# Joining a head's attention and carry products, and loading the Nyquist weights with a repeated source

## The chip, the cores and the metric

The kernel runs on one core of a Trainium2 chip. The metric is the device time of one execution in microseconds (us). Engines are called TensorE (PE in the profile, its weight loads PEld), VectorE (DVE), ScalarE (ACT), GpSimd (POOL) and SyncE (SP, whose queue issues nearly all DMAs).

## The reference

One layer of a diffusion backbone for 128 context tokens and 256 latent tokens, width 2048, all in float32. Cut to what matters here:

```python
# adaLN: shift, scale and gate vectors from SiLU(cond) @ w_ada, for both sub-layers
h = rmsnorm(x, norm_pre_mix) * (1 + sc1) + sh1
q, k, v, g, lr_f, lr_b, fo = split(h @ w_in)
# branch A: gated linear attention, 4 heads, both directions, in chunks of 64 tokens
b = cumsum(log_a); total = b[last]
q_in, k_in, k_out = q * exp(b), k * exp(-b), k * exp(total - b)
att = where(mask, q_in @ k_in.T, 0)         # within a chunk
o = att @ v + q_in @ state                  # state carried from chunk to chunk
state = state * exp(total) + k_out.T @ v
# branch B: real part of a 2-D DFT over positions and the 256 channels of each of 4 groups
f = fft2(fo.reshape(t, 4, 256), axes=(positions, channels)).real
merged = sigmoid(gate_a) * (norm(o) * silu(g) @ w_br_gla) + sigmoid(gate_b) * (f @ w_br_four)
x = x + ga1 * rmsnorm(merged @ w_out)
x = x + ga2 * rmsnorm(swiglu_ffn(rmsnorm(x) * (1 + sc2) + sh2))
# outputs: x of both token kinds, and the final context states of both directions
```

## The kernel before

All 384 tokens go through the layer together, and activations lie transposed: channels on partitions, tokens in the free dimension. A large product is done as three float32r products of split operands (high x high, high x low, low x high). The helper `gemm` issues them (line 257), 24 for a weight tile of 128 x 1024. Such a tile is loaded by SP (`load`, L196, tile raw, 2 buffers), and split by `split`: ScalarE copies the high part (L224, whi), VectorE subtracts the low part (L225, wlo), 4 buffers each. `grab` takes a finished tile and starts the load and split of a later one. `proj` makes one output tile of 128 channels from two weight tiles, and after each of the two it calls `step(side)`, which runs one piece of side work up to its next `yield`. The order on TensorE, ScalarE, VectorE and GpSimd is the order of the program (`manual_schedule`); the order of SP's queue is left to the scheduler until the last stage.

The stages that the change touches are two.

**GLA.** While the 32 gate projections run, the side work is `gla()` with the generator `ada_rest` beside it, one step of each after every weight tile. `ada_rest` multiplies the remaining adaLN weights on VectorE (L530, tile adacc, about 2.5 us a step); every 18 steps it has two products on TensorE: pr (L538) and, one step later, ptm (L547). For each of 4 heads, `gla` makes kr, the decay exponents (z, la, bT, sx), per direction d the tiles qi, ki, ko, kc (VectorE, L661 to L668), and then in three steps: the attention products of direction 0 (at, L684), those of direction 1 (at again), and the carry products from chunk to chunk (cr, L704). Each of these is 6 small products with 64 output rows, plain float32, so that the profile shows 12 records of each. VectorE copies at under a mask into att (L687), for direction 1 by way of the tile am (L694, L697), and ScalarE copies cr into att (L708). Later steps split att, ko and q, and make the state products dl and the outputs po. All of these results lie in the PSUM pool `pss` of 5 tiles (tag side), which are handed out in turn.

**Fourier branch.** After GLA, 8 projections make the Fourier channels (fo), two for each of 4 groups. The second of a pair makes sum and difference of both (fs, VectorE, L898 and L899). The side work `dft()` then does the DFT over channels with the constants cd: px (L844, L845) one step later, then pp (L830). The Nyquist channel has its own row pnr and its own weights wn, which `four` uses (L943) once for each of 16 output tiles. wn holds 128 x 2048 values, of which rows 0 to 3, 32 to 35 and 64 to 67 are filled: the same four weight rows three times, as high, low and high part. `nyq_weights(h)` makes one half: GpSimd clears a tile wr (L868), SP loads its 12 rows by 12 DMAs (L873), each 8 pieces of 128 floats; in the next step ScalarE copies wr to wn (L876) and VectorE subtracts for the low rows (L877). wr shares its buffer (tag ws, one buffer) with the tile in which `fold` adds up the weights of `w_br_four`. After each of the first four projections one step of it is run.

Of the kernel before, what the change touches and what calls it, by code (L numbers as in the profile page):

```python
# [11 lines left out]
F32 = mybir.dt.float32  # L12
# [8 lines left out]
P = 128  # L21
# [5 lines left out]
CH = 64  # L27
# [69 lines left out]
def tile_step(ctx: ExitStack, tc: tile.TileContext, a, o):  # L97
    nc = tc.nc
    PE, ACT, DVE, POOL, SP = nc.tensor, nc.scalar, nc.vector, nc.gpsimd, nc.sync
# [215 lines left out]
    pss = ctx.enter_context(tc.tile_pool(name="pss", bufs=5, space=PSUM))  # L315
    with ExitStack() as s:
# [126 lines left out]
        for kb in range(KT):  # L443
# [17 lines left out]
            hf = scr[:, kb % 8, :]  # L461
# [42 lines left out]
        for t in range(3):  # L504
# [5 lines left out]
            for g in range(2):  # L510
                cs = slice(512 * g, 512 * g + 512)
# [58 lines left out]
    with ExitStack() as s:  # L570
        pg = s.enter_context(tc.tile_pool(name="pg", bufs=1))
# [8 lines left out]
        for c in range(2):  # L580
            src = a["a2"][:, 512 * c : 512 * c + 512]
# [3 lines left out]
        mask = pg.tile([P, 2, CH], U32, name="mask")  # L585
        ss = pg.tile([P, 3, 4], F32, name="ss")

        def hf(c):
            return slice(64 * (c % 2), 64 * (c % 2) + 64)
# [4 lines left out]
        def gla():  # L594
# [10 lines left out]
            for h in range(NH):  # L605
# [33 lines left out]
                for d in range(2):  # L639


                    bT = pss.tile([P, T], F32, tag="side", name="bT")
                    for t in range(3):
                        for j, l in enumerate((lah, lal)):
                            PE.matmul(
                                bT[:, t * P : (t + 1) * P], l[:, t, d], tri[:, d * P : (d + 1) * P],
                                start=j == 0, stop=j == 1,
                            )
                    sx = pss.tile([P, 2, P], F32, tag="side", name="sx")
                    for j, l in enumerate((lah, lal)):  # L650
                        PE.matmul(
                            sx, tri[:, (2 + d) * P : (3 + d) * P], l[:, 0 : 2 + d : 1 + d, d], start=j == 0, stop=j == 1,
                        )
                    eb = pg.tile([P, T], F32, tag=f"eb{d}", name="eb")
                    ACT.activation(eb, bT, AF.Exp)
                    ki = pg.tile([P, T], F32, tag=f"ki{d}", name="ki")
                    ACT.activation(ki, bT, AF.Exp, scale=-1.0)
                    ko = pg.tile([P, 2, P], F32, tag=f"ko{d}", name="ko")
                    ACT.activation(ko, sx, AF.Exp)
                    qi = pg.tile([P, T], F32, tag=f"qi{d}", name="qi")  # L660
                    DVE.scalar_tensor_tensor(qi, eb, DK**-0.5, qT[:, h, :], op0=ALU.mult, op1=ALU.mult)  # L661
                    DVE.tensor_mul(ki, ki, kT[:, h, :])
                    DVE.tensor_mul(ko, ko, krs[:, 0 : 2 + d : 1 + d, :])

                    last = 0 if d else CH - 1
                    tot = chunks(eb)[:, :, d, last : last + 1]
                    kc = pg.tile([P, 3, CH], F32, tag=f"kc{d}", name="kc")
                    DVE.tensor_mul(kc, chunks(ki)[:, :, d, :], tot.to_broadcast([P, 3, CH]))  # L668
                    dc = pg.tile([P, 1], F32, tag=f"dc{d}", name="dc")
                    c = 5 if d else 2  # L670
                    e0, e1 = c * CH + last, (c + 1 - 2 * d) * CH + last
                    DVE.tensor_mul(dc, eb[:, e0 : e0 + 1], eb[:, e1 : e1 + 1])
                    qin.append(qi)
                    kin.append(ki)
                    kcr.append(kc)
                    kout.append(ko)
                    dec.append((tot, dc))
                    yield
                for d in range(2):
                    qi, ki = qin[d], kin[d]  # L680
                    at = pss.tile([P, 3, CH], F32, tag="side", name="at")
                    for c in range(6):
                        cs = slice(c * CH, (c + 1) * CH)
                        PE.matmul(at[hf(c), c // 2, :], ki[:, cs], qi[:, cs], start=True, stop=True)  # L684
                    if d == 0:
                        for c in range(2):
                            DVE.copy_predicated(  # L687
                                att[hf(c), :, c * CH : (c + 1) * CH],
                                mask[hf(c), 0:1, :].to_broadcast([CH, 3, CH]), at[hf(c)],
                            )  # L690
                    else:
                        am = pg.tile([P, 3, CH], F32, tag="am", name="am")
                        POOL.memset(am, 0.0)
                        DVE.copy_predicated(am, mask[:, 1:2, :].to_broadcast([P, 3, CH]), at)  # L694
                        for c in range(2):
                            v = att[hf(c), :, c * CH : (c + 1) * CH]
                            DVE.tensor_add(v, v, am[hf(c)])  # L697
                    yield

                cr = pss.tile([P, 3, CH], F32, tag="side", name="cr")  # L700
                for t in range(3):
                    for d in range(2):
                        c = 2 * t + 1 - d
                        PE.matmul(  # L704
                            cr[hf(d), t, :], kcr[d][:, t, :], qin[d][:, c * CH : (c + 1) * CH], start=True, stop=True,
                        )
                for d in range(2):
                    ACT.copy(att[hf(d), :, (1 - d) * CH : (2 - d) * CH], cr[hf(d)])  # L708
                for d in range(2):
# [93 lines left out]
    with ExitStack() as s:  # L803
# [57 lines left out]
            DVE.tensor_sub(pnr[64:96], pn[64:96], pnr[64:96].bitcast(F32))  # L861
            yield

        def nyq_weights(h):

            n = D // 2
            wr = pc.tile([P, n], F32, tag="ws", name="wr")
            POOL.memset(wr, 0.0)  # L868
            for g in range(4):
                src = a["w_br_four"][8 * h : 8 * h + 8, 32 * g : 32 * g + 1, (2 * g + 1) * P : (2 * g + 2) * P]  # L870
                for j in range(3):
                    r = 32 * j + g
                    SP.dma_start(wr[r : r + 1, :].rearrange("p (i c) -> p i c", c=P), src.rearrange("i p c -> p i c"))  # L873
            yield
            w = wn[:, n * h : n * h + n]
            ACT.copy(w, wr)  # L876
            DVE.tensor_sub(w[32:64], wr[32:64], w[32:64].bitcast(F32))  # L877
            yield

        df = dft()  # L880

# [4 lines left out]
                yield  # L886

        sd = side()
        nw = (u for h in range(2) for u in nyq_weights(h))
        rate[0] = 0.7  # L890
        for i in range(8):
            def fo(p, i=i):
                if i % 2 == 0:
                    fs[i // 2] = pc.tile([P, 2, T], F32, tag="fs", name="fs", bufs=2)
                    ACT.copy(fs[i // 2][:, 0, :], p)
                else:
                    f = fs[i // 2]
                    DVE.tensor_sub(f[:, 1, :], f[:, 0, :], p)  # L898
                    DVE.tensor_add(f[:, 0, :], f[:, 0, :], p)  # L899
                    done[0] = i + 1  # L900

            proj(psm, hT, fo, sd)
            if i < 4:
                next(nw)

        gates, raw_gates = {}, []
        gorder = iter([u for u in mix_order if u[0] != "o"])
# [424 lines left out]
```

## Time and profile before

| what | value |
|---|---|
| time, median of 3 runs | 2057.03 us (2055.79 to 2059.26) |
| the profiled execution's own time | 2056.04 us |
| its span, first to last instruction | 2054.3 us |
| TensorE busy | 2024.7 us, 99% of the span |
| VectorE, ScalarE, GpSimd busy | 1274.9, 770.1, 45.4 us |
| granted TensorE clock | 0.994 of full speed |
| GLA heads lie in | about 200 to 480 us |
| Fourier projections lie in | about 510 to 590 us |

A row of a timeline gives start, length, engine, line, operation, output and inputs, count, and in brackets how long the engine sat idle before it and what ended that. Matmuls are pipelined, so their lengths overlap; what one costs is read from start to start. A row of a tile or line gives the count, least, median and greatest length in ns, and the first and last start. SPq is the time in which SP issues a DMA.

### The profile page before, as it was taken

The numbers are of one execution on the slowest core, as the hardware profiler recorded it, in microseconds if no ns is written. First come the engines' busy times: TensorE is split into PE (matmuls) and PEld (weight loads), VectorE is DVE, ScalarE is ACT, GpSimd is POOL, SyncE is SP. The second block draws the span as 40 slices with busy tenths as digits, with TensorE's granted clock in tenths as the row PEclk, the third lists the DMA queues.
The fourth block names the chain that finished last, engine by engine and source line by source line (L and its number), as shares of the span: only waits on it lengthen the run. The fifth ranks groups of instructions, "written<-read, shape, count | busy, mean of one in ns | idle before, by whom it ended". The sixth has DMA issues, their size and how long they took to land.

```text
span 2054.3 us, 30097 instructions
## 1 busy us (share of the span) xinstructions
PE 2024.7 (99%) x12214; PEld 1956.1 (95%) x12214; DVE 1274.9 (62%) x1663; ACT 770.1 (37%) x1143; POOL 45.4 (2%) x52
## 2 busy tenths in 40 slices
PE   8999999999999999999999999999999999999998
PEld 5779999999999999978999999999999999999996
DVE  5669787898667778867444555553545454544346
ACT  3233545453346544445333322222222322222234
POOL 0000000000000000022000000000000000000001
PEclk9999999999999999999999999999999999999998
DMA  9978677767646785532444444443444444433332
GB/s 387 354 261 274 206 238 230 240 222 259 202 158 209 257 282 183 187 113 93 154 144 152 146 144 154 144 146 125 150 144 147 151 144 148 148 125 124 123 133 83
DMA packets 112563, 373.94 MB, mean 182 GB/s; under 512 B 13860, under 2 KB 32484, under 8 KB 108328
## 3 DMA queue, kind: packets, MB, share of 16 engines
q1 hardware_dynamic: 111560, 370.84, 52.8%
q8 instruction: 96, 1.57, 0.3%
q10 hardware_dynamic: 864, 1.18, 0.2%
q14 instruction: 43, 0.35, 0.1%
HBM read 358.34 MB, written 13.63 MB: 181 GB/s over the span
## 4 chain that ended last, share of the span: by engine, by line
PE 96%; DVE 2%; DMA 1%; ACT 1%; issue 0%; SPq 0%; DVEq 0%; ACTq 0%
PE pmm L257 66%; PE pdn L257 18%; PE pv L391 3%; PE pf L257 2%; PE pgm L374 1%; PE px L409 1%; DVE yE L1227 0%; PE po L603 0%; PE pmm L1131 0%; DMA Clo<-in_xT 0%; PE pr L538 0%; DMA slab<-in_w_ada 0%; DVE z L1090 0%; PE dl L603 0%; PE px L844 0%
## 5 line engine op out<-in xcount | busy, mean ns | idle before, releaser
L257 PE MATMUL pmm<-A_hi,whi 128*128 128x384 f32 x2480 | 832.6, 336 | 0.0
L257 PE MATMUL pmm<-A_hi,wlo 128*128 128x384 f32 x2480 | 828.9, 334 | 0.0
L257 PE MATMUL pmm<-A_lo,whi 128*128 128x384 f32 x2480 | 828.8, 334 | 0.0
L225 DVE TENSOR_TENSOR wlo<-raw,whi 128x1024 fp32r<-128x1024 f32 x433 | 529.0, 1223 | 433.8 <-ACT whi L224 432.9
L224 ACT CAST whi<-raw 128x1024 fp32r<-128x1024 f32 x436 | 457.7, 1050 | 587.4 <-PE pmm L257 223.2
L257 PEld LDWEIGHTS pmm<-A_hi,whi 128*128 128x128 f32 x2480 | 465.6, 188 | 3.4 <-issue 1.8
L257 PEld LDWEIGHTS pmm<-A_lo,whi 128*128 128x128 f32 x2480 | 465.7, 188 | 0.2
L257 PEld LDWEIGHTS pmm<-A_hi,wlo 128*128 128x128 f32 x2480 | 465.6, 188 | 0.0
L530 DVE SCALAR_TENSOR_TENSOR adacc<-adaw,spad,adacc 128x1024 f32<-128x1024 f32 x240 | 296.9, 1278 | 0.6 <-DMA adaw<-in_w_ada 0.3
L257 PE MATMUL pdn<-hid_hi,whi 128*128 128x384 f32 x704 | 235.2, 334 | 0.0
L257 PE MATMUL pdn<-hid_hi,wlo 128*128 128x384 f32 x704 | 235.1, 334 | 0.0
L257 PE MATMUL pdn<-hid_lo,whi 128*128 128x384 f32 x704 | 235.1, 334 | 0.0
L257 PEld LDWEIGHTS pdn<-hid_hi,whi 128*128 128x128 f32 x704 | 132.2, 188 | 0.4 <-issue 0.4
L257 PEld LDWEIGHTS pdn<-hid_lo,whi 128*128 128x128 f32 x704 | 132.2, 188 | 0.0
L257 PEld LDWEIGHTS pdn<-hid_hi,wlo 128*128 128x128 f32 x704 | 132.2, 188 | 0.0
L283 ACT CAST hid_hi<-hfE 128x384 fp32r<-128x384 f32 x44 | 22.6, 513 | 161.6 <-DVE hfE L1154 161.6
L1154 DVE TENSOR_TENSOR hfE<-sg,pmm 128x384 f32<-128x384 f32 x44 | 24.4, 555 | 82.2 <-PE pmm L257 81.6
L1146 ACT ACTIVATE sg<-pmm 128x384 f32<-128x384 f32 x44 | 21.6, 492 | 133.5 <-PE pmm L257 133.5
L1171 DVE TENSOR_TENSOR Blo<-Blo,pdn 128x384 f32<-128x384 f32 x72 | 39.5, 553 | 46.6 <-PE pdn L257 46.6
L1171 DVE TENSOR_TENSOR Bhi<-Bhi,pdn 128x384 f32<-128x384 f32 x72 | 39.0, 549 | 34.0 <-PE pdn L257 34.0
L257 PE MATMUL pmm<-o_hi,whi 128*128 128x384 f32 x128 | 42.8, 335 | 0.0
L257 PE MATMUL pmm<-o_lo,whi 128*128 128x384 f32 x128 | 42.8, 334 | 0.0
(301 smaller groups left out, 1556.9 us busy)
## 6 DMA issues: line engine op xcount, KB each, us to landing
adaw<-in_w_ada SPq DMA_DIRECT2D x128, 512.0 KB
raw<-in_w_g SPq DMA_DIRECT2D x88, 512.0 KB
raw<-in_w_u SPq DMA_DIRECT2D x88, 512.0 KB
raw<-in_w_d SPq DMA_DIRECT2D x88, 512.0 KB
slab<-in_w_ada SPq DMA_DIRECT2D x32, 1024.0 KB
raw<-in_w_gate SPq DMA_DIRECT2D x64, 512.0 KB
raw<-in_w_in SPq DMA_DIRECT2D x44, 512.0 KB
raw<-in_w_out SPq DMA_DIRECT2D x32, 512.0 KB
```

The costliest lines, as they stand in the source:

```text
L224: ACT.copy(hi, raw)
L225: eng.tensor_sub(lo, raw, hi.bitcast(F32))
L257: PE.matmul(dst, w[wi][:, k * n + n0 : k * n + n0 + P], x[xi][:, k0 + k, :], start=first and k == 0 and j == 0, stop=last and k == kts - 1 ...
L283: ACT.copy(hi, src)
L374: PE.matmul(pgv[q : q + 32, :], spad[:, k, :], slab[k // (KT // 2)][:, k % (KT // 2), :], start=k < 4, stop=k >= KT - 4,)
L391: PE.matmul(pv[2 * t + g], hT[x_][:, kb, t * P : (t + 1) * P], w_[:, g * 512 : (g + 1) * 512], start=kb == 0 and j == 0, stop=kb == KT - 1 ...
L409: PE.matmul(px, w_[:, u * P : (u + 1) * P], hT[x_][:, kb, :], start=j == 0, stop=j == 2)
L530: DVE.scalar_tensor_tensor(acc[:, c, :], w, spad[:, k, c : c + 1], acc[:, c, :], op0=ALU.mult, op1=ALU.add,)
L1146: ACT.activation(sgs[j], p, AF.Silu)
L1154: DVE.tensor_mul(hf, sgs.pop(j), p)
L1171: DVE.tensor_add(acc(k), acc(k), p)
```

## The change

In `gla`, the 12 attention products of both directions and the 6 carry products are issued in one step, one after the other on TensorE. The work of the other engines on them keeps its three steps; the number of steps of a head stays the same. In the Fourier branch, each half of the Nyquist weights is loaded by four DMAs, each of which reads a weight row once for each of three target rows 32 partitions apart (a source with a repeated dimension). Two of them are issued in one step and two in the next, and the copy follows in a third, so that both halves take six steps, after the first six projections.

```diff
@@ -676,26 +676,13 @@
                     kout.append(ko)
                     dec.append((tot, dc))
                     yield
+
+                ats = []
                 for d in range(2):
-                    qi, ki = qin[d], kin[d]
-                    at = pss.tile([P, 3, CH], F32, tag="side", name="at")
+                    ats.append(pss.tile([P, 3, CH], F32, tag="side", name="at"))
                     for c in range(6):
                         cs = slice(c * CH, (c + 1) * CH)
-                        PE.matmul(at[hf(c), c // 2, :], ki[:, cs], qi[:, cs], start=True, stop=True)
-                    if d == 0:
-                        for c in range(2):
-                            DVE.copy_predicated(
-                                att[hf(c), :, c * CH : (c + 1) * CH],
-                                mask[hf(c), 0:1, :].to_broadcast([CH, 3, CH]), at[hf(c)],
-                            )
-                    else:
-                        am = pg.tile([P, 3, CH], F32, tag="am", name="am")
-                        POOL.memset(am, 0.0)
-                        DVE.copy_predicated(am, mask[:, 1:2, :].to_broadcast([P, 3, CH]), at)
-                        for c in range(2):
-                            v = att[hf(c), :, c * CH : (c + 1) * CH]
-                            DVE.tensor_add(v, v, am[hf(c)])
-                    yield
+                        PE.matmul(ats[d][hf(c), c // 2, :], kin[d][:, cs], qin[d][:, cs], start=True, stop=True)
 
                 cr = pss.tile([P, 3, CH], F32, tag="side", name="cr")
                 for t in range(3):
@@ -704,6 +691,19 @@
                         PE.matmul(
                             cr[hf(d), t, :], kcr[d][:, t, :], qin[d][:, c * CH : (c + 1) * CH], start=True, stop=True,
                         )
+                for c in range(2):
+                    DVE.copy_predicated(
+                        att[hf(c), :, c * CH : (c + 1) * CH],
+                        mask[hf(c), 0:1, :].to_broadcast([CH, 3, CH]), ats[0][hf(c)],
+                    )
+                yield
+                am = pg.tile([P, 3, CH], F32, tag="am", name="am")
+                POOL.memset(am, 0.0)
+                DVE.copy_predicated(am, mask[:, 1:2, :].to_broadcast([P, 3, CH]), ats[1])
+                for c in range(2):
+                    v = att[hf(c), :, c * CH : (c + 1) * CH]
+                    DVE.tensor_add(v, v, am[hf(c)])
+                yield
                 for d in range(2):
                     ACT.copy(att[hf(d), :, (1 - d) * CH : (2 - d) * CH], cr[hf(d)])
                 for d in range(2):
@@ -861,21 +861,24 @@
             DVE.tensor_sub(pnr[64:96], pn[64:96], pnr[64:96].bitcast(F32))
             yield
 
-        def nyq_weights(h):
+        def nyq_weights():
 
             n = D // 2
-            wr = pc.tile([P, n], F32, tag="ws", name="wr")
-            POOL.memset(wr, 0.0)
-            for g in range(4):
-                src = a["w_br_four"][8 * h : 8 * h + 8, 32 * g : 32 * g + 1, (2 * g + 1) * P : (2 * g + 2) * P]
-                for j in range(3):
-                    r = 32 * j + g
-                    SP.dma_start(wr[r : r + 1, :].rearrange("p (i c) -> p i c", c=P), src.rearrange("i p c -> p i c"))
-            yield
-            w = wn[:, n * h : n * h + n]
-            ACT.copy(w, wr)
-            DVE.tensor_sub(w[32:64], wr[32:64], w[32:64].bitcast(F32))
-            yield
+            for h in range(2):
+                wr = pc.tile([P, n], F32, tag="ws", name="wr")
+                POOL.memset(wr, 0.0)
+                for g in range(4):
+                    src = a["w_br_four"][8 * h : 8 * h + 8, 32 * g : 32 * g + 1, (2 * g + 1) * P : (2 * g + 2) * P]
+                    SP.dma_start(
+                        wr[g : g + 65 : 32, :].rearrange("p (i c) -> p i c", c=P),
+                        src.rearrange("i p c -> p i c").to_broadcast([3, 8, P]),
+                    )
+                    if g % 2:
+                        yield
+                w = wn[:, n * h : n * h + n]
+                ACT.copy(w, wr)
+                DVE.tensor_sub(w[32:64], wr[32:64], w[32:64].bitcast(F32))
+                yield
 
         df = dft()
 
@@ -886,7 +889,7 @@
                 yield
 
         sd = side()
-        nw = (u for h in range(2) for u in nyq_weights(h))
+        nw = nyq_weights()
         rate[0] = 0.7
         for i in range(8):
             def fo(p, i=i):
@@ -900,8 +903,7 @@
                     done[0] = i + 1
 
             proj(psm, hT, fo, sd)
-            if i < 4:
-                next(nw)
+            next(nw, None)
 
         gates, raw_gates = {}, []
         gorder = iter([u for u in mix_order if u[0] != "o"])
```

## The prediction

> **What bounds the kernel now.** I read the page first, for the bound.
>
> ```profile
> span 2054.3 us, 30097 instructions
> PE 2024.7 (99%) x12214; PEld 1956.1 (95%) x12214; DVE 1274.9 (62%) x1663; ACT 770.1 (37%) x1143; POOL 45.4 (2%) x52
> ```
>
> TensorE is busy 99% of the span. So an edit pays only where it takes time out of TensorE's own row: instructions that go, a pause between instructions, or a wait. Work taken from SP, VectorE, ScalarE or GpSimd pays nothing unless TensorE waits for it. The question for each half of the change is therefore what TensorE loses at that place today.
>
> For the Fourier projections I read the chain of waits from 500 to 605 us. Its columns are start, length, what.
>
> ```profile
> 526.99 1.34 issue
> 528.33 0.67 PE px L844 x2
> ...
> 530.67 4.19 PE pmm L257 x24
> ...
> 548.69 0.43 PE px L844 x2
> ...
> 550.66 4.17 PE pmm L257 x24
> ```
>
> Before the first px group the chain has a hole of 1.34 us; the second group has none. Hole and group take 530.67 - 526.99 = 3.68 us the first time, 550.66 - 548.69 = 1.97 us the second. The first occurrence costs 1.71 us extra. The timelines of SP, ScalarE, VectorE and TensorE, in that order, say why.
>
> ```profile
> 513.33 8.06 SPq L873 DMA_DIRECT2D wr<-in_w_br_four  x12
> 521.49 2.10 SPq L196 DMA_DIRECT2D raw<-in_w_in  x2
> 528.17 0.90 SPq L915 DMA_DIRECT2D gate<-gates_d  x2
> 525.45 1.05 ACT L224 CAST whi<-raw 128x1024 fp32r<-128x1024 f32 x1 [9.36 <-DMA raw<-in_w_in]
> 526.54 1.23 DVE L225 TENSOR_TENSOR wlo<-raw,whi 128x1024 fp32r<-128x1024 f32 x1 [6.79 <-ACT whi L224]
> 527.68 0.54 DVE L898 TENSOR_TENSOR fs<-fs,pmm 128x384 f32<-128x384 f32 x1
> 528.33 0.67 PE L844 MATMUL px<-cd,fs 128*128 128x257 f32 x2 [1.34 <-issue]
> ```
>
> SP issues twelve small loads in a row, 8.06 us, and only then the weight load at 521.49. ScalarE waits 9.36 us for that load, VectorE 6.79 us for ScalarE, and the fs subtraction stands behind that split in VectorE's queue. It ends at 528.22; px starts at 528.33. The row calls the wait "issue", but the queue ahead of fs shows it to be a late load.
>
> For the GLA heads I read TensorE's timeline around the attention products of head 1 (at at 295.23, cr at 304.96), twice more cut off inside the at group, and around the second at group of head 0.
>
> ```profile
> 294.79 0.33 PE L257 MATMUL pmm<-A_lo,whi 128*128 128x384 f32 x1
> 294.96 0.34 PE L257 MATMUL pmm<-A_hi,wlo 128*128 128x384 f32 x1
> 295.23 0.57 PE L684 MATMUL at<-qi,ki 128*64 128x64 f32 x12
> 295.73 0.45 PE L257 MATMUL pmm<-A_hi,whi 128*128 128x384 f32 x1
> 296.01 0.34 PE L257 MATMUL pmm<-A_lo,whi 128*128 128x384 f32 x1
> ...
> 304.70 0.34 PE L257 MATMUL pmm<-A_hi,wlo 128*128 128x384 f32 x1
> 304.96 0.57 PE L704 MATMUL cr<-qi,kc 128*64 128x64 f32 x12
> ...
> 305.75 0.34 PE L257 MATMUL pmm<-A_lo,whi 128*128 128x384 f32 x1
> ```
>
> ```profile
> 295.23 0.34 PE L684 MATMUL at<-qi,ki 128*64 128x64 f32 x4
> ```
>
> ```profile
> 295.23 0.51 PE L684 MATMUL at<-qi,ki 128*64 128x64 f32 x10
> ```
>
> ```profile
> 232.70 0.34 PE L257 MATMUL pmm<-A_hi,wlo 128*128 128x384 f32 x1
> 232.97 0.57 PE L684 MATMUL at<-qi,ki 128*64 128x64 f32 x12
> 233.47 0.44 PE L547 MATMUL ptm<-ident,adev 128*128 128x128 f32 x2
> ...
> 233.93 0.34 PE L257 MATMUL pmm<-A_lo,whi 128*128 128x384 f32 x1
> ```
>
> Projection products follow each other by 294.96 - 294.79 = 0.17 us. From the last one ahead of the at group to the second one behind it, 294.96 to 296.01 is 1.05 us; two ordinary steps are 0.35, so the group costs 0.70 us. cr reads the same: 305.75 - 304.70 - 0.35 = 0.70. Inside, the records run much faster. The window that was cut at 295.36 holds 4 records, the one cut at 295.53 holds 10: six in 0.17 us, 0.029 us each. Twelve records at that rate are 0.35 us. The other 0.35 us is a price per group: 0.10 before it (295.23 - 294.96 - 0.17), a slow first pair and an emptying at its end, and 0.11 more on the product that follows (296.01 - 295.73 - 0.17).
>
> **GLA: three groups in one.** No instruction goes. Per head, 36 records in three groups become 36 in one: 36 x 0.029 + 0.35 = 1.40 us, against 3 x 0.70 = 2.10. That is 0.70 us saved in an undisturbed head. In head 0 the shared side generator already puts its own plain float32 products straight behind the at groups (pr behind the first, ptm behind the second). The number of steps stays the same, so pr will still join the one group, while ptm loses its companion. at with ptm costs 233.93 - 232.70 - 0.35 = 0.88, so ptm adds 0.18 behind at; alone it costs between 0.18 and 0.18 + 0.35. I take 0.33, since it keeps the full column width and so should miss part of that price, and head 0 saves 0.55. Together: 3 x 0.70 + 0.55 = 2.65 us, with 2.5 and 2.8 as ends if nothing waits.
>
> What can wait is the moved part: the second at needs ki of direction 1, and cr needs kc, in the step just after VectorE makes them; until now cr came two steps later.
>
> ```profile
> 294.68 0.35 DVE L668 TENSOR_TENSOR kc<-ki,eb 128x192 f32<-128x192 f32 x1
> ```
>
> kc of direction 1 ends at 295.03 in head 1, 0.20 us before the first at begins (295.23). In the joined group cr begins 24 records later: 295.23 + 24 x 0.029 + 0.05 for the slow first pair, about 295.98. The margin is 0.9 us, and ki, made before kc, has more. So I put this wait at nothing; VectorE's own work up to kc covers it, and a delay of kc beyond 0.9 us would be paid by TensorE one to one, with every weight product behind it in TensorE's queue. The other moves are free: the predicated copies, the additions, the copy of cr and the scaling of q keep their steps on VectorE and ScalarE, and their operands only come earlier. GpSimd's clearing of am moves past nothing. The three groups hold three of the five PSUM tiles of the side pool at once; what they take over are the tiles of z, bT and sx, which were read a step before. What is late next after this saving are the state products (dl), whose operands VectorE splits; they come 0.7 us sooner against a VectorE queue that is 62% busy over the span.
>
> **Nyquist weights: four loads a half, in two units.** Twelve loads become four, so a half costs SP four issues in place of twelve, and between the two units a whole projection's loads may go out.
>
> ```profile
> L873 SPq DMA_DIRECT2D wr<-in_w_br_four x24: 620/621/737, 513.3 to 538.4; - x24
> L584 SPq DMA_DIRECT2D raw<-in_a x2: 281/304/326, 146.5 to 148.7; - x2
> ```
>
> A load of this shape takes SP 0.62 us, and 8.06 / 12 = 0.67 with the gap to the next. A load with three target rows and a repeated source is not in the trace. The nearest from below is L584, which also repeats its source, over two partitions: 0.30. From above it is three of today's loads, 3 x 0.67 = 2.0 us. I take 0.67, since L584 shows that a repeated source need not cost more. Two loads then hold SP for 1.3 us, four for 2.7. SP's order is not written out by hand here, and the gate loads at 528.17, which the program places after all eight projections, show that SP takes what is ready; so the second unit's loads may follow the first at once, and the spreading may not be seen. Even then the weight load behind them goes out 8.06 - 2.7 = 5.4 us sooner than at 521.49, and ScalarE, VectorE and fs move up with it. px needs only 1.71 us of that, and then starts behind its projection, as the second group does. So the gain is 1.71 us; even 1.58 us a load, (8.06 - 1.71) / 4, would give all of it.
>
> The second half's loads moved SP alike (the same 0.62 us each), but TensorE shows no hole there, so nothing is gained. The copy and the subtraction that make wn move from after projections 2 and 4 to after 3 and 6. They are two instructions each on ScalarE and VectorE as before, and their cover is the lead that wn has:
>
> ```profile
> L943 PE MATMUL pf<-edT,wn x16: 268/273/277, 607.0 to 710.5; 96*128 96x194 f32 x16
> ```
>
> Two projections take about 20 us (px at 528.33 and 548.69), so the sixth ends before the fourth px group at about 588, and wn is first read at 607.0. On GpSimd the second clearing waits for that subtraction, one projection later than today, with nothing but itself behind it; on SP the loads behind the clearing would wait with it if it were late.
>
> **The sum.** 2.65 + 1.71 = 4.36 us. Both savings sit in TensorE's row and everything after is fed by the same queues in the same order, so I let them through whole. The profiled execution took 2056.04 us (span 2054.3 and 1.74 around it): 2056.04 - 4.36 = 2051.68. The median of the runs is 0.99 above it, so the forecast is 2052.7 us, or 0.21% less.
>
> **The rivals.**
>
> A late raw load meets the joined group (slower). In VectorE's order the split of a weight tile stands right ahead of qi, ki and kc, and it waits for ScalarE, which waits for a load:
>
> ```profile
> ACT whi L224 <- DMA raw<-in_w_gate: 53.1, 27, 5.0
> ```
>
> Such waits came 27 times, the longest 5.0 us. If one of that length fell on this step in each head, kc would be late by 5.0, and cr, which used to have two more steps of about 4.9 us, only has the margin of 0.9: 4 x (5.0 - 0.9) = 16.4 us lost, less the 4.36, so 2069.1 us. It decides from 0.9 + 4.36 / 4 = 2.0 us of lateness in every head. For it speaks that the slack is given up; against it that VectorE shows no such idle time before qi in head 1 and that a tile is split several products ahead of its use. Chance 0.08.
>
> The loads on few DMA engines keep the stall. A load with three rows outermost may be carried by three of the sixteen engines, eight rows of 512 bytes each, where a raw load behind it must pass.
>
> ```profile
> q1 hardware_dynamic: 111560, 370.84, 52.8%
> ```
>
> A packet took 0.528 x 16 x 2054.3 / 111560 = 0.156 us on average, so 8 x 0.156 = 1.25 us a load and 5.0 us for four in a row. The raw load would go out 5.4 us sooner and land up to 5.0 later on those engines: 0.4 us of the 1.71 is won, and the time is 2057.03 - 2.65 - 0.4 = 2054.0. The average packet holds 370.84 MB / 111560 = 3.3 KB, so 512 bytes should take much less; that speaks against it. Chance 0.10. The Trainium skill states the rule in "DMA: Bandwidth & Descriptors", section "Rules for kernel authors": a leading zero-stride broadcast of c copies confines the whole load to at most c engines. It speaks against this form of load. By that rule this rival's time follows if the packets take their mean; no row so far shows which engines carry such a load.
>
> The joined group saves nothing. If the 0.35 us were not a price per group but went with the records (the accumulator tile changes twice inside the group), or if VectorE stayed the pace of the heads, only the Fourier stall goes: 2057.03 - 1.71 = 2055.3. For it speaks that no row shows more than twelve such records in a row; against it that the next product is slowed by 0.11 after each group and that the records inside run at a constant rate. Chance 0.12.
>
> **How the numbers follow.** The forecast has 0.70. About 0.2% (4.1 us) is what a measurement of this kernel can tell from no change, and the forecast lies only just beyond it. Of its 0.70 I count 0.53 beyond that bound and 0.17 within. The second and third rivals lie within it (0.22), and of the slower one 0.06 beyond and 0.02 within. So 0.53 faster, 0.41 same, 0.06 slower. The runs of before lie 3.47 us apart (2055.79 to 2059.26), so half of that, 1.74, stands on each side of a median. Downward: 2052.7 - 0.15 (head 0 saves the whole 0.70) - 1.74 = 2050.8. Upward the range takes in the third rival with 1.3 of the 1.74: 2056.6. What is left out is the slower rival and the tails.
>
> **What would show it.** TensorE's timeline should hold one group of 36 records per head, costing about 1.40 us between its neighbours, with no idle time inside it; a gap before the records of cr refutes the margin. The chain should show no hole before the first px group, and 1.97 us for it. SP should issue four loads per half of 0.3 to 2.0 us each, in one run or two, and the weight load behind them by about 516. The forecast is wrong if the heads' span or the stretch from 500 to 605 us keeps its length, or if a new wait on TensorE appears later.

## The result, and the profile after

| what | before | after |
|---|---|---|
| median | 2057.61 us (10 runs, 2055.79 to 2059.34) | 2052.81 us (10 runs, 2051.47 to 2054.36) |
| ratio | | 0.9975, 95% interval 0.9966 to 0.9985 |
| the profiled execution | 2056.04 us, span 2054.3 | 2051.67 us, span 2049.9 |

The changed kernel is faster by 0.25%, with 0.15% and 0.34% as ends: the middle lies beyond the 0.2% of the prediction, the near end within it. A repetition (e10 below) gave 0.9979. The page still shows TensorE as the bound:

```profile
span 2049.9 us, 30068 instructions
PE 2019.5 (99%) x12214; PEld 1954.7 (95%) x12214; DVE 1275.6 (62%) x1663; ACT 769.6 (38%) x1143; POOL 45.3 (2%) x52
q1 hardware_dynamic: 111392, 370.84, 52.8%
```

The same 12214 matmuls take TensorE 5.2 us less busy time, and there are 29 instructions fewer. The busy row alone measures little: in the second profile of the same kernel (e10) it is 2022.4 us, only 2.3 less, with a span 3.2 us shorter than before. The third line answers to the queue row of the prediction: the same bytes in 168 packets fewer, which is used further down.

The chain of waits has no "issue" row ahead of the first px group any more:

```profile
524.30 0.43 PE px L844 x2
...
526.27 4.17 PE pmm L257 x24
...
544.27 0.43 PE px L844 x2
...
546.24 4.17 PE pmm L257 x24
```

Both groups now take 1.97 us (526.27 - 524.30 and 546.24 - 544.27); before, the first took 3.68 with its hole. SP's timeline shows why:

```profile
510.97 1.62 SPq L872 DMA_DIRECT2D wr<-in_w_br_four  x2
512.72 0.35 SPq L196 DMA_DIRECT2D raw<-in_w_in  x1
513.11 1.49 SPq L872 DMA_DIRECT2D wr<-in_w_br_four  x2
514.71 0.35 SPq L196 DMA_DIRECT2D raw<-in_w_in  x1
```

Two loads, a weight load, two loads, a weight load. The next weight load goes out at 512.72, between the two units, and the one behind all four at 514.71; in the kernel before, the next one stood behind all twelve and went out at 521.49.

TensorE's timeline of head 1 holds one group where there were three:

```profile
294.41 0.34 PE L257 MATMUL pmm<-A_hi,wlo 128*128 128x384 f32 x1
294.68 0.92 PE L685 MATMUL at<-qi,ki 128*64 128x64 f32 x24
295.43 0.52 PE L691 MATMUL cr<-qi,kc 128*64 128x64 f32 x12
...
296.16 0.34 PE L257 MATMUL pmm<-A_lo,whi 128*128 128x384 f32 x1
```

From the last product ahead to the second one behind, less two ordinary steps: 296.16 - 294.41 - 0.35 = 1.40 us, with no idle time in brackets. Three groups cost 2.10.

The gain can be located to a few hundredths, since the first record of bT in head 0 and the first px group bracket the two stages. That record of the kernel before, and of the changed one:

```profile
215.86 0.33 PE L645 MATMUL bT<-cg,lah 128*128 128x128 f32 x1
```

```profile
215.96 0.33 PE L645 MATMUL bT<-cg,lah 128*128 128x128 f32 x1
```

| stage | before | after | difference |
|---|---|---|---|
| first instruction to this bT | 215.86 | 215.96 | +0.10 |
| bT to the first px group or its hole | 526.99 - 215.86 = 311.13 | 524.30 - 215.96 = 308.34 | -2.79 |
| the hole and the group | 3.68 | 1.97 | -1.71 |
| behind it to the end | 2054.3 - 530.67 = 1523.6 | 2049.9 - 526.27 = 1523.6 | 0.0 |

The sum is -4.40 us, the difference of the spans. All of the gain lies in the two edited places, and nothing was given back behind them.

### The profile page after: what moved, and what is told of

It is laid out like the page before. It is cut to its first block, busy times and chain, and to the rows that moved or that the text cites. A ratio compares the mean times of both kernels' runs of the same rounds, so it can differ in the third digit from the quotient of the medians.

```text
span 2049.9 us, 30068 instructions
## 1 busy us (share of the span) xinstructions
PE 2019.5 (99%) x12214; PEld 1954.7 (95%) x12214; DVE 1275.6 (62%) x1663; ACT 769.6 (38%) x1143; POOL 45.3 (2%) x52
## 3 DMA queue, kind: packets, MB, share of 16 engines
q1 hardware_dynamic: 111392, 370.84, 52.8%
## 4 chain that ended last, share of the span: by engine, by line
PE 96%; DVE 3%; ACT 1%; issue 1%; DMA 0%; SPq 0%; DVEq 0%; ACTq 0%
PE pmm L257 66%; PE pdn L257 18%; PE pv L391 3%; PE pf L257 2%; PE pgm L374 2%; PE px L409 1%; DVE yE L1229 0%; PE po L603 0%; PE pr L538 0%; DVE z L1092 0%; DMA Chi<-in_xT 0%; PE dl L603 0%; PE pgm L472 0%; DVE z L1086 0%; DVE A_lo L1105 0%
```

## The experiments

Two questions were open after this: whether each edit alone gives its part, and by which of its features. The theory: the GLA edit saves a price per group of small products, 0.35 us each, and the load edit takes SP time from ahead of a weight load. The rivals: the saving belongs to something else in the edits (the order of cr, the spreading, the repeated source), and the three slower or smaller outcomes of the prediction. The edits are cut to what matters, with `...` for what is left out. Those of e1, e3, e4, e7, e9 and e11 are shown against the changed kernel, those of e5 and e6 against the kernel before; what a heading says in brackets comes on top.

**e1: the joined group with the twelve loads of before.**

```diff
-        def nyq_weights():
+        def nyq_weights(h):
...
-                    SP.dma_start(
-                        wr[g : g + 65 : 32, :]..., src....to_broadcast([3, 8, P]),
-                    )
-                    if g % 2:
-                        yield
+                for j in range(3):
+                    r = 32 * j + g
+                    SP.dma_start(wr[r : r + 1, :]..., src...)
```

> Theory: the two savings are independent and add up. One group of 36 records per head, the twelve Nyquist loads as before: the heads get 2.77 us shorter (0.70 in heads 1 to 3, 0.66 in head 0), the hole ahead of the first px group stays at 1.3 us in the chain, and the time is 2.8 us below the kernel before, ratio 0.9987. Rival: the heads are paced by VectorE, and the 4.4 us come from the Fourier stretch and elsewhere; then the end of the last head moves by less than 1 us and the ratio is 0.9995 or more.

Measured: 2055.39 us (11 runs) against 2057.08 (33 runs), ratio 0.9991 (0.9983 to 1.0). The heads came out as expected (1.40 each, 2.39 and 0.22 in head 0), but the hole grew. The chain of e1, and the window of 526 to 536 us of the kernel before and of e1 (columns: window, length, busy time of PE, PEld, DVE, ACT and POOL, granted clock, DMA share, GB/s):

```profile
525.65 2.06 issue
527.71 0.67 PE px L844 x2
...
530.68 5.18 PE pmm L257 x24
```

```profile
526.00:536.00 10.00, 8.66 (x55) 7.99 (x53) 8.39 (x9) 6.28 (x15) 0.96 (x1) 1.00 0.59 198
```

```profile
526.00:536.00 10.00, 8.29 (x39) 7.81 (x40) 8.13 (x8) 5.01 (x13) 0.95 (x1) 0.83 0.49 184
```

TensorE is done with the products ahead 1.34 us earlier (525.65 against 526.99), the weight load behind the twelve comes only 0.61 us earlier (ScalarE starts on it at 524.84 against 525.45), and the hole is 2.06 us in place of 1.34. Behind it the granted clock is 0.83 where it was 1.00, the group needs 530.68 - 527.71 = 2.97 us in place of 2.34, and the next 24 products 5.18 in place of 4.19. So in this execution some 2.3 us (0.72 + 0.63 + 0.99) of the GLA gain was lost at the stall that the other edit removes. It is the longest of e1's eleven executions (2057.63 us; the shortest took 2053.05), so how much is lost as a rule isn't known. The hole grows in e3 too, by less (hole and group 3.86 us against 3.68). The medians don't decide it: e1 is 1.69 us below the kernel before (0 to 3.5 by its interval) and e2, which follows, 2.60, together 4.29, about the whole of the change. That the load edit also keeps what the GLA edit gains is therefore shown by single executions only.

**e2: the new loads with the three steps of before** (the reverse of e1).

> Theory: the four loads in two units take the hole away and nothing else: 1.71 us below the kernel before, ratio 0.9992; heads unchanged at three groups of 0.70. Rival: the hole only went because TensorE came to it 2.8 us earlier or later in another phase with the loads; then the hole stays with the heads as before, and the ratio is 1.000.

Measured: 2054.48 us against the same 2057.08, ratio 0.999 (0.9981 to 0.9999). The px group takes 530.25 - 528.28 = 1.97 us and has no hole; the heads keep their three groups of 0.70:

```profile
528.28 0.43 PE px L844 x2
...
530.25 4.17 PE pmm L257 x24
```

**e3: two groups, at with at, and cr two steps later** (twelve loads as before).

```diff
                         PE.matmul(ats[d][hf(c), c // 2, :], ...)
-                cr = ...  # with its products
                 for c in range(2):
                     DVE.copy_predicated(...)
                 yield
...
                 yield
+                cr = ...  # with its products
```

> The two attention groups joined, the carry products two steps later as before, the twelve loads as before. Theory (a price of 0.35 us per group of plain float32 products): two groups of 24 and 12 records per head cost 1.05 and 0.70, so 0.35 us is saved per head and about 1.4 us in all, half of the saving of one group; ratio 0.9993. Rival: the price is one of the change of shape between attention and carry products or of the records themselves; then the group of 24 costs 1.40 and nothing is saved.

Measured: 2055.17 us, ratio 0.9992 (0.9983 to 1.0). The interval alone decides nothing; TensorE's timeline of head 1 does:

```profile
294.30 0.34 PE L257 MATMUL pmm<-A_hi,wlo 128*128 128x384 f32 x1
294.57 0.92 PE L685 MATMUL at<-qi,ki 128*64 128x64 f32 x24
...
295.69 0.34 PE L257 MATMUL pmm<-A_lo,whi 128*128 128x384 f32 x1
```

24 records cost 295.69 - 294.30 - 0.35 = 1.04 us. With 12 at 0.70 and 36 at 1.40, each twelve records add 0.35 us, and what is left over is 0.35 whatever the size. It is a price per group, and it doesn't matter which of the attention and carry products share it.

**e4: twelve loads as before, six in one unit and six in the next** (GLA of before).

```diff
-                    SP.dma_start(wr[g : g + 65 : 32, :]..., src....to_broadcast([3, 8, P]))
+                    for j in range(3):
+                        r = 32 * j + g
+                        SP.dma_start(wr[r : r + 1, :]..., src...)
                     if g % 2:
                         yield
```

> The heads as before; the Nyquist weights by twelve loads a half, without repeated source, but in six units (six loads in each of two). Theory (what counts is the SP time ahead of the next raw load): if the scheduler lets a raw load go out between the units, as it did in the changed kernel, six loads hold it for 4.0 us in place of 8.06 and the hole is gone: 1.7 us below the kernel before, ratio 0.9992. Rival: the number of loads or the repeated source is what counts; then a hole of about 1.3 us stays and the ratio is 1.000.

Measured: 2055.42 us, ratio 0.9992 (0.9983 to 1.0001). SP's timeline:

```profile
515.04 4.07 SPq L874 DMA_DIRECT2D wr<-in_w_br_four  x6
519.21 0.37 SPq L196 DMA_DIRECT2D raw<-in_w_in  x1
519.64 3.96 SPq L874 DMA_DIRECT2D wr<-in_w_br_four  x6
```

The weight load goes out between the units, and the px group takes 1.97 us without a hole. The repeated source isn't needed for the gain.

**e5: four repeated loads in one unit** (GLA of before).

```diff
-                for j in range(3):
-                    r = 32 * j + g
-                    SP.dma_start(wr[r : r + 1, :]..., src...)
+                SP.dma_start(wr[g : g + 65 : 32, :]..., src....to_broadcast([3, 8, P]))
```

> The heads as before; each half by four loads with repeated source, all four in one unit, placed as the twelve were. Theory: four loads at the 0.77 us that a pair of them showed hold SP for 3.1 us in place of 8.06, the raw load goes out 5 us sooner, and the first px group costs 1.97 us with no hole: the spreading is not needed. Rival (the loads crowd onto three DMA engines and hold the raw load up there): a hole is left, and ScalarE still waits several us for the raw load.

Measured in a single run: 2055.89 us against 2058.11 (19 runs). Four loads in a row hold SP 3.11 us, 0.78 each, and the px group again takes 530.29 - 528.32 = 1.97 us:

```profile
515.52 3.11 SPq L871 DMA_DIRECT2D wr<-in_w_br_four  x4
518.74 0.83 SPq L196 DMA_DIRECT2D raw<-in_w_in  x2
```

So neither feature of the load edit is needed if the other is there. What counts is how long SP is held ahead of the weight load: 8.06 us is too long; 4.07 and 3.11 are not.

**e6: twelve loads with a repeated source in one unit** (GLA of before; 36 rows are filled, and the added ones meet zeros).

```diff
-                    r = 32 * j + g
-                    SP.dma_start(wr[r : r + 1, :]..., src...)
+                    r = 4 * j + g
+                    SP.dma_start(wr[r : r + 65 : 32, :]..., src....to_broadcast([3, 8, P]))
```

> The heads as before; twelve loads with repeated source a half, in one unit placed as before (each source row goes to three times as many rows; the added rows meet zeros). Theory: the hole follows SP's time one to one. 12 x 0.77 = 9.2 us in place of 8.06 puts the raw load 1.2 us later, so the hole grows from 1.3 to about 2.5 us and hole and first px group cost 4.9 us in place of 3.68. Rival (engines): 12 loads of eight rows in turn on three engines are up to 15 us there; the raw load lands far later than SP's delay explains, and the hole is over 4 us.

Measured in a single run: 2056.86 us against the same 2058.11. The timelines of SP and ScalarE, the chain, and the queue row of the page:

```profile
513.55 9.08 SPq L873 DMA_DIRECT2D wr<-in_w_br_four  x12
522.74 0.83 SPq L196 DMA_DIRECT2D raw<-in_w_in  x2
```

```profile
526.18 1.05 ACT L224 CAST whi<-raw 128x1024 fp32r<-128x1024 f32 x1 [10.13 <-DMA raw<-in_w_in]
```

```profile
526.94 2.11 issue
...
531.40 4.19 PE pmm L257 x24
```

```profile
q1 hardware_dynamic: 111824, 371.03, 53.7%
```

SP is held 9.08 us, 1.02 more than by the twelve plain loads, and hole and group take 531.40 - 526.94 = 4.46, which is 0.78 more. That is less than the 4.9 that was expected with a hole that follows SP's time one to one. The weight load needs 526.18 - 522.74 = 3.44 us from issue to ScalarE's start; behind twelve plain loads it needed 525.45 - 521.49 = 3.96. In the changed kernel, behind two repeated loads, it needed 3.39 (512.72 to 516.11). So twelve repeated loads ahead of it don't delay it on the DMA engines; SP's time explains the longer hole, and the quicker arrival is why it grew by less than SP's time.

**e7 and e8: qi of direction 1 computed three times more**, so that ki and kc come later; e7 on the changed kernel, e8 on the new loads with the three steps of before.

```diff
                     DVE.scalar_tensor_tensor(qi, eb, DK**-0.5, qT[:, h, :], ...)
+                    for _ in range(3 * d):
+                        DVE.scalar_tensor_tensor(qi, eb, DK**-0.5, qT[:, h, :], ...)
```

> The changed kernel, with the product that makes qi of direction 1 done three times more on VectorE ahead of ki and kc (same values): ki and kc come 3 x 0.47 = 1.4 us later in each head. Theory (cr in the joined group has a margin of 0.96 us, at of direction 1 about 1.2): TensorE stalls 0.2 us before the second at and 0.5 us in all before cr, about 2 us over the four heads against the changed kernel. Rival: VectorE is not that close, and the stall is nothing; or VectorE's queue then makes the state products late too, and it is over 4 us.

> The same three added products of 1.4 us a head in the kernel with three groups and the new weight loads. Theory: cr comes two steps, 9.7 us, after the first at and hides them; no wait of TensorE in the heads that was not there, and the time of that kernel without them (about 1.7 us below the kernel before) stays within 0.5 us. Rival: the added work fills VectorE and the state products wait, 0.5 us or more a head, in both kernels alike.

Measured: e7 2056.07 us, ratio 0.9995 (0.9985 to 1.0005); e8 2054.76, ratio 0.9986 (0.9977 to 0.9995), both against 2058.11. VectorE's and TensorE's timelines of e7 in head 1:

```profile
294.00 0.55 DVE L661 SCALAR_TENSOR_TENSOR qi<-eb,qk 128x384 f32<-128x384 f32 x1
294.58 1.74 DVE L663 SCALAR_TENSOR_TENSOR qi<-eb,qk 128x384 f32<-128x384 f32 x3
296.25 0.55 DVE L664 TENSOR_TENSOR ki<-ki,qk 128x384 f32<-128x384 f32 x1
```

```profile
295.82 0.57 PE L687 MATMUL at<-qi,ki 128*64 128x64 f32 x12
296.95 0.57 PE L687 MATMUL at<-qi,ki 128*64 128x64 f32 x12 [0.56 <-DVE ki L664]
297.32 0.70 PE L693 MATMUL cr<-qi,kc 128*64 128x64 f32 x12
```

From qi to ki it is 296.25 - 294.00 = 2.25 us, where it is 0.47 in the changed kernel (292.85 to 293.32): ki and kc come 1.78 us later, more than the 1.4 intended. The second at group waits for ki, which ends at 296.25 + 0.55 = 296.80; the row of cr, 0.70 long in place of 0.52, suggests that it waited a little for kc too. The groups of heads 1 to 3 cost 2.32 to 2.33 us in place of 1.40, and TensorE's stretch from bT to px is 312.10 us, 3.76 more than in the changed kernel (about 2 were expected, for 1.4 us of lateness). In e8 the same lateness costs nothing: that stretch is 311.11, as in the kernel before, and TensorE's only wait between 200 and 480 us is the one for lal that all these kernels have. So the slack that the change gives up is real, and 1.78 us of lateness is already more than it holds.

**e9: one more step in head 0**, ahead of bT, against that wait for lal.

```diff
                 split_act(lah, lal, la)
+                if h == 0:
+                    yield
```

> The changed kernel with one empty step more in head 0, after the decay exponents are split (lah, lal). Theory: the one wait that TensorE has left in the heads, before the first bT group of head 0 (that group costs 2.05 us there and 0.90 elsewhere), is the time that VectorE and ScalarE need for lal after their activation tables are loaded; a step of 4.2 us of projections covers it, the group costs 0.90, and 1.15 us go, less up to 0.2 because pr and ptm then meet other groups: about 1.0 us below the changed kernel, ratio to the kernel before 0.9970. Rival: the wait moves with the step, or the shifted side work makes a new one; then nothing is gained.

Measured: 2068.24 us (5 runs) against 2057.98, ratio 1.0053 (1.0039 to 1.0067). It was expected to gain 1 us and lost 14.8 against the changed kernel (2053.47 in e10, beside it). TensorE's waits between 200 and 480 us of the changed kernel and of e9 (columns: us in total, times, longest):

```profile
PE bT L645 <- DVE lal L284: 0.7, 1, 0.7
```

```profile
PE bT L647 <- ACT lah L283: 6.8, 3, 2.3
PE bT L647 <- DVE lal L284: 2.0, 3, 0.7
```

Head 0 has lost its wait, and heads 1 to 3 have each got a longer one. ScalarE's timelines of the changed kernel and of e9 at the second head say why:

```profile
275.97 0.58 ACT L794 ACTIVATE gz<-pmm,bgate 128x384 f32<-128x384 f32 x1 [2.68 <-PE pmm L257]
277.39 0.87 ACT L631 ACTIVATE la<-z 128x512 f32<-128x512 f32 x2
```

```profile
283.55 0.58 ACT L796 ACTIVATE gz<-pmm,bgate 128x384 f32<-128x384 f32 x1 [3.25 <-PE pmm L257]
284.03 0.86 ACT L631 ACTIVATE la<-z 128x512 f32<-128x512 f32 x2
```

A gate projection has two halves, and ScalarE reads it out (gz) after the second. One step more puts the heads on the other half: the exponents la now stand right behind a gz that waited 3.25 us for TensorE, though the products z that they are made from were done about 4 us before (they start at 278.83), and bT needs them in the next step. The windows of e9 around the three waits show what else it cost:

```profile
286.00:300.00 14.00, 11.06 (x59) 10.60 (x58) 11.08 (x16) 9.23 (x14) 0.00 (x0) 0.88 0.29 98
358.00:372.00 14.00, 11.06 (x59) 10.60 (x58) 10.42 (x14) 9.24 (x14) 0.00 (x0) 0.88 0.26 87
431.00:446.00 15.00, 12.05 (x57) 11.59 (x56) 10.97 (x15) 8.76 (x14) 0.00 (x0) 0.77 0.22 74
```

The waits add 6.8 + 2.0 - 0.7 = 8.1 us; a granted clock of 0.88, 0.88 and 0.77 over these windows (1.00 in the changed kernel) is worth about 0.12 x 14 + 0.12 x 14 + 0.23 x 15 = 6.8. Together 14.9, against the 14.8.

**e10: the changed kernel again**, beside e9.

> The changed kernel again, for the comparison on the same chip: 4.4 us below the kernel before, ratio 0.9979; joined groups of 1.40 us, no hole before the first px group.

Measured: 2053.47 us (11 runs), ratio 0.9979 (0.9971 to 0.9988); the joined group costs 1.40 and the px group 1.97 again.

**e11: e9 with a second extra step at the end of head 0**, so that heads 1 to 3 fall back on their own half.

```diff
                 split_act(lah, lal, la)
+                if h == 0:
+                    yield
...
+                if h == 0:
+                    yield
```

> One empty step after the decay exponents of head 0 and a second one at the end of head 0, so that heads 1 to 3 keep their place against the two halves of a gate projection. Theory (with one added step, ScalarE had to do the gate copy gz, which waits for the end of the projection, ahead of the exponents of heads 1 to 3): the waits of 2.3 us before bT in heads 1 to 3 are gone, those groups cost 0.90 again, and head 0 keeps its gain: bT, pr, at with cr and ptm cost 0.90 + 2.11 + 1.58 = 4.59 in place of 2.05 + 0.90 + 2.39 + 0.22 = 5.56, 1.0 us below the changed kernel, ratio to the kernel before 0.997 to 0.9975. Rival: the added steps make the heads late as such (VectorE's order against TensorE's); then waits stay in heads 1 to 3 and the time is above the changed kernel.

Measured: 2051.65 us (5 runs) against 2058.2, ratio 0.9966 (0.9952 to 0.998). TensorE has no wait left between 200 and 480 us, and bT with sx costs about 0.9 us in every head. It is the lowest of all medians here, 0.13% below the changed kernel by the two ratios, though their intervals overlap. It agrees with the reading of e9: the loss came from which half of a projection the heads fall on, not from a step as such.

The stages of the other kernels, by the same records as above (the bT record, the first px row or hole, the products behind it, the span):

| kernel | to bT | bT to px | hole and px | behind it |
|---|---|---|---|---|
| e1 | 217.30 | 308.35 | 5.03 | 1525.1 |
| e2 | 217.16 | 311.12 | 1.97 | 1524.0 |
| e3 | 215.48 | 309.76 | 3.86 | 1523.6 |
| e4 | 216.97 | 311.12 | 1.97 | 1523.5 |
| e6 | 215.83 | 311.11 | 4.46 | 1523.7 |
| e10 | 217.22 | 308.33 | 1.97 | 1523.6 |

The stretch with the heads repeats to 0.02 us between kernels with the same GLA code, and e3 lies 1.37 below before, about four times 0.35. Apart from the hole of e1 and what follows it, what moves between executions lies ahead of bT (215.48 to 217.30), where nothing was edited.

## Why the prediction was right

**The bound.** Only TensorE's own row was counted, and the table of stages bears it out: the two terms appear whole in the span, 4.50 us together against the 4.36 of the sum, with 0.10 more ahead of bT. That the measured median, 2052.81, lies so close to the forecast of 2052.7 is in part luck: the kernel before has 2057.61 in the ten runs beside it, 0.58 above the median that the forecast started from, and the difference of the medians is 4.80, not 4.36. In the sets of runs here the median of the kernel before lies anywhere from 2057.03 to 2058.20; the stages say it more sharply.

**The GLA term.** It was 2.65 us, and 2.79 came out. The undisturbed heads were put at 1.40 for the joined group and measured 1.40, 1.40 and 1.39. Head 0 was mis-sized: ptm without its companion was taken at 0.33 and costs 0.22. In TensorE's timeline of the changed kernel it is 234.06 - 233.49 - 0.35:

```profile
233.49 0.34 PE L257 MATMUL pmm<-A_hi,wlo 128*128 128x384 f32 x1
233.67 0.38 PE L547 MATMUL ptm<-ident,adev 128*128 128x128 f32 x2
...
234.06 0.34 PE L257 MATMUL pmm<-A_lo,whi 128*128 128x384 f32 x1
```

It was 0.18 behind at, so this pair of full column width pays hardly any price of its own (0.04, not 0.15). Head 0 therefore saves 0.66, not 0.55.

**The margin.** It was put at 0.9 us for cr, read from the start of at and a rate of 0.029 us a record. In VectorE's timeline of the changed kernel

```profile
294.12 0.35 DVE L668 TENSOR_TENSOR kc<-ki,eb 128x192 f32<-128x192 f32 x1
```

ends at 294.47 and cr starts at 295.43: 0.96. e7 weighs it: 1.78 us of lateness cost 0.92, so 0.86 was hidden. ki does have more margin, as the prediction says: 1.78 late, it was waited for by 0.56, which leaves 1.22. It is only waited for first because the second at group comes ahead of cr.

**The Nyquist term.** 1.71 us, and 1.71 came out (3.68 - 1.97). The 0.37 us of it that lies behind the hole is the same wait: L845 needs the second fs (L899), which VectorE ended at 528.26 + 0.55 = 528.81, and it starts at 528.87. That the "issue" row was really a late weight load is shown by e4 and e5, which shorten only SP's time ahead of that load and lose the hole, and by e6, which lengthens it and gets a longer one. The price of a load was taken at 0.67 us and is 0.78 with its gap (3.11 / 4 in e5), well inside the 0.30 to 2.0 given. Whether the spreading would be seen was left open; it was: a weight load went out between the units.

**The rivals.** That the joined group saves nothing (price with the records) is refuted by e3. The late operand that meets the joined group is a true mechanism by e7 and e8, but its condition doesn't occur: TensorE's only wait in the heads is the old one for lal. That the loads' three engines keep the stall is half true. Each plain load counts y packets and each repeated one x: 24 plain loads against 8 repeated ones make 111392 - 111560 = -168 = 8x - 24y, and in e6 111824 - 111560 = 264 = 24x - 24y. So x is 27 and y is 16, where both kinds have 8 pieces of data a row: 24 + 3 and 8 + 8. The records of the packets bear this out: of 512 bytes there are 192 in the kernel before, 192 in the changed one and 576 in e6, and the rest, three or eight a load, are packets of 4 bytes. If that rest is one packet for each engine used, a repeated load runs on three engines and a plain one on eight. That agrees with the rule of the Trainium skill, "DMA: Bandwidth & Descriptors", section "Rules for kernel authors". The delay that the rival built on it isn't there: a weight load behind twelve such loads took 3.44 us to arrive, not more than the 3.96 behind plain ones. The step that fell is its packet price: 0.156 us was the mean over packets of 3.3 KB, and these hold 512 bytes; in the trace of the changed kernel their median is 0.027 us, so the eight of a load on one engine take about 0.2 us, less than the 0.78 in which SP issues it.

## What to carry to other kernels

Small products in another form between large ones can cost TensorE a fixed price for each group: here 0.35 us for those of 64 output rows, and 0.04 for a pair of full width. Put those that pay it into one group where their operands are ready, and measure the margin by delaying an operand on purpose. A cheap transfer isn't free when it stands in front of a large one on the issuing queue: twelve loads of 0.67 us were worth 1.71 us of TensorE, and either fewer of them or a place for the large load between them was enough. Where side work is dealt out in steps, a step more or less can move all that follows to the other half of a projection; look at what then stands ahead of it on each engine.

## What the runs showed of the hardware

A short stall can cost more than its length. Behind the hole of 2.06 us in e1 the granted clock was 0.83 over 10 us, and a narrower window shows what this mean is made of (columns as above):

```profile
529.30:532.70 3.40, 3.40 (x12) 3.22 (x12) 3.37 (x4) 2.56 (x9) 0.95 (x1) 0.50 0.49 173
```

It is half speed for 3.4 us, with 1.00 on either side, and so a loss of 1.7 us. In e9, behind pairs of waits of about 2.3 and 0.7 us, the clock is 0.50 from 292.6 to 296.0, from 364.3 to 367.7 and from 436.0 to 442.8: once, once and twice 3.4 us. The Trainium skill, "TensorE: Matmul & The Clock Gate", Part 1, "The HAM clock gate", states such a gate: half rate, decided in free-running windows of about 3.4 us, after a window of idleness. The rate and the length agree with the traces; that a whole idle window is needed doesn't, as the holes here were shorter. Nor does length alone decide it: behind the 2.11 us of e6 the clock stayed at 1.00, and the next 24 products took 4.19 us, as usual. By that rule of the Trainium skill it would be the phase that decides. No experiment sets the phase, and what the traces show of it is mixed. If windows of 3.41 us are counted on from the half-speed stretches of the same trace, e1's hole lies almost whole in one window (TensorE idle for about 1.8 us of it) and e6's is split over two (about 0.9 and 1.2). But in e9 a window with about 1.5 us idle (285.8 to 289.2) was followed by full speed and the next one, with 1.4, by half. It stays open.

A load with a repeated source and three target rows takes SP 0.71 to 0.85 us, little more than the 0.62 of one row, though it writes three times as much:

```profile
L872 SPq DMA_DIRECT2D wr<-in_w_br_four x8: 709/733/853, 511.0 to 540.5; - x8
```

Products on VectorE that write the same tile again follow each other in 0.58 us (294.58 - 294.00 in e7), where qi and ki, two tiles of the same size, follow each other in 0.47 (292.85 to 293.32 in the changed kernel); that is why e7 was later than intended.
